# A tiny transfer out of the newest accumulated weight tile, put ahead of the transposing transfer of each feed-forward block

## The chip, the core and the metric

The program runs on one core of one Trainium2 chip. The metric is device time in microseconds (us): 1848.22 us, the median of three runs of the kernel before (1848.09, 1848.22 and 1849.85).

## What is computed

A two-layer encoder over 512 tokens of width 1024, in float32. Each layer adds half a gated feed-forward (width 2816) to x, then a mixer, then half a second feed-forward; a last norm closes it.

```python
def swiglu(x, w_in, w_out):
    gu = x @ w_in
    g, u = jnp.split(gu, 2, axis=-1)
    return (jax.nn.silu(g) * u) @ w_out

for l in range(DEPTH):
    x = x + 0.5 * swiglu(rms_norm(x, ffn1_norm[l]), ffn1_w_in[l], ffn1_w_out[l])
    x = x + mixer(rms_norm(x, mix_norm[l]), ...)
    x = x + 0.5 * swiglu(rms_norm(x, ffn2_norm[l]), ffn2_w_in[l], ffn2_w_out[l])
return rms_norm(x, final_norm)
```

The change lies in the four feed-forwards alone. The mixer (attention over a neighbourhood, a Fourier mix and their gates) has the same code before and after.

## The kernel before

**Products.** A product in float32 is made of three matmuls, on operands split into a high and a low part (`whi`, `wlo` for weights, `xh`, `xl` and the like for activations). ACT makes the high part (L191, L186), DVE the low part (L194, L187), TensorE multiplies (L514, L515, L517).

**Blocks.** The first half of a feed-forward works through the hidden width in five blocks (`NB`) of 512 columns (the first feed-forward has a plain part ahead of them; the other three begin with `first_block`, which carries 256 extra columns). A block is a two by two scheme of the Strassen and Winograd kind with seven products, in the order 1, 5, 6, 2, 7, 3, 4. Its four weight quarters are called a, b, c and d; a and b belong to the gate, c and d to the other factor. Products 5 and 7 want sums of quarters, d+c and c+a. The second half of the feed-forward (the output stage, tiles `o`) multiplies by the second weight matrix in the same scheme, in three chunks.

**Weights.** A quarter comes in two granules of 128 x 1024 (512 KB). `Raw.load` asks for a granule: SP issues the plain load into a `raw` tile (L148), and where a sum is wanted, GpSimd (POOL) issues an accumulating load of the second quarter into the same tile (L150), which has to wait until the plain load has landed. Below, "accumulating load" means the latter. The list of granules is fixed; `Stream` keeps eight of them (`FETCH`) asked for ahead of the last one that is split, and splits two (`AHEAD`) ahead of the product that is being issued. Nine `raw` buffers are in use.

**The hidden tile.** A block gives two half tiles of the hidden activation, `z2` (tokens 256 to 511) and `z1` (tokens 0 to 255), which are needed transposed. ACT pulls the two 16-bit words of each number apart into `zs` (`words_apart`, L350); SP issues a transposing transfer from `zs` to `zt` (`turned_words`, L356); one block later ACT joins the words into `at` (`joined_words`, L369), the one of `z2` after product 6, the one of `z1` after product 7. So SP's queue holds plain loads and transposing transfers, in an order that the scheduler made from the program, and each row of it waits on SP for its semaphores before it is issued; what stands behind it waits too.

**The function that the change replaces.** In `stage_ffn` the transposing transfer of `z2` stands under `with behind_sums(...)`. That function looks up the second granule of quarter c of the next block in the table `sums`; if that granule has been asked for, it issues a transfer of 16 numbers out of its tile to DRAM (tile `seen`), and `tc.issue_after` keeps what is issued under the `with` behind that transfer on the queue. Where the granule has not been asked for yet (`raw.t is None`), it does nothing. In the program as built, no row of SP's queue writes `seen`.

Of the kernel before, what the change touches and what calls it, by code (L numbers as in the profile page):

```python
# [9 lines left out]
F32 = mybir.dt.float32  # L10
# [81 lines left out]
def encoder_kernel(  # L92
    ctx: ExitStack, tc: tile.TileContext, xin, xtr, wst, gains, gfin, gbias, bias_in, dft, chan, ident_in, rot, out
):
    nc = tc.nc
# [8 lines left out]
    dp = ctx.enter_context(tc.tile_pool(name="dp", bufs=2, space=bass.MemoryType.DRAM))  # L104
# [3 lines left out]
    def nm(s):  # L108
        uid[0] += 1
        return f"{s}_{uid[0]}"  # L110

    def slot(dt=F32, s="k", shape=(4, 256)):
        return kp.tile([P, *shape], dt, tag="k", name=nm(s), bufs=23)
# [25 lines left out]
    class Raw:  # L139
# [3 lines left out]
        def load(self, parts=1):  # L143
            if self.t is None:
                self.t = raw_pool[0](self.n)
                for c in range(0, self.n, self.n // parts):
                    cs = slice(c, c + self.n // parts)
                    nc.sync.dma_start(out=self.t[:, cs], in_=wst[GRAN_AT[self.key]][:, cs])  # L148
                if self.plus:
                    G.dma_start(out=self.t, in_=wst[GRAN_AT[self.plus]][:, 0 : self.n], accum_op=ALU.add)  # L150

    class Item:
# [43 lines left out]
                G.dma_start(out=t, in_=wst[GRAN_AT[self.then]][:, 0:n], accum_op=ALU.add)  # L196
            self.out = (hi, lo)

    sums = {}

    def stage_items():
        items, st = [], 0

        def add(*a, **k):
            items.append(Item(*a, stage=st, **k))

        def strassen(s, name, idx, sizes, order, dma=False, behind=None):
            def key(q, g):
                return (s, name(q), idx, g) if g < 2 else (s, "h" + q, idx, 0)

            r = {}
            for q, q2 in (("a", None), ("b", None), ("c", "a"), ("d", "c")):
                r[q] = [Raw(key(q, g), n, q2 and key(q2, g)) for g, n in enumerate(sizes)]
                sums.update({z.key: z for z in r[q] if z.plus})
            d2 = [Raw(key("d", g), n) for g, n in enumerate(sizes)]
            at = [(m, g) for m in order for g in range(len(sizes))]
            if len(sizes) == 3:
                at.remove((2, 2))
                at.insert(at.index((7, 2)), (2, 2))
            for m, g in at:  # L220
                a, b, c, d = [r[q][g] for q in "abcd"]
                if m == 1:
                    add(a, neg=True)
                elif m == 2:
                    add(b)
                elif m == 3:
                    add(d, None if dma else b)
                elif m == 4:
                    add(d2[g])
                elif m == 5:  # L230
                    add(d)
                elif m == 6:
                    add(d, a, then=b.key if dma else None)
                else:
                    add(c)
                for key in (behind or {}).get(m, ()) if g == len(sizes) - 1 else ():
                    add(Raw(key))

        def out_sizes(c):
            return (1024, 512) if c == 0 else (1024, 1024)  # L240

        def ffn(s):
            first = not items
            if first:
                for g in range(4):
                    add(Raw((s, "cl", g)), parts=2 if g < 2 else 1, pieces=2 if g == 0 else 1)
            for j in range(NB):
                order = (1, 2, 5, 6, 7, 3, 4) if first and j == 0 else (1, 5, 6, 2, 7, 3, 4)
                strassen(s, lambda q: q, j, (1024,) * (2 if first or j else 3), order)
            for order in ((1,), (2,), (5, 6, 7, 3), (4,)):  # L250
                for c in range(3):
                    summed = s == (L - 1, 2) and c == 2
                    strassen(s, lambda q: "o" + q, c, out_sizes(c), order, summed)

        for l in range(L):
            ffn((l, 1))
            st += 1
            s = (l, 0)
            two = (1024, 1024)
            qk = [(s, "qk", g) for g in range(8)]  # L260
            strassen(s, lambda q: "u" + q, 0, two, (1, 5, 6, 2, 3, 7, 4), True, behind={5: qk[0:1], 6: qk[1:2], 2: qk[2:3], 3: qk[3:4], 7: qk[4:5]})
            for key in qk[5:] + [(s, "f", g) for g in range(4)]:
                add(Raw(key))
            st += 1
            for g in range(2):
                add(Raw((s, "n", 0, g)))
            st += 1
            for i in range(2):
                strassen(s, lambda q: "g" + q, i, two, ORDER, True)
            for g in range(2):  # L270
                add(Raw((s, "n", 1, g)))
            strassen(s, lambda q: "w" + q, 0, two, ORDER, True)
            ffn((l, 2))
        return items
# [78 lines left out]
    def turned_words(s):  # L353

        t = slot(U16, "zt", (2, 4, 256))
        nc.sync.dma_start_transpose(  # L356
            out=t.rearrange("p h q (b t) -> p (h q b) t", b=2), in_=s.rearrange("p h q b f -> p (h q b f)")
        )
        return t

    def apart(z):

        return turned_words(words_apart(z))
# [257 lines left out]
    def stage_ffn(norm, nxt, late):  # L621

        hx, lx = norm.h, norm.l
        stage = (norm.idx // 3, 1 + (norm.idx % 3) // 2)
        at = {}

        def at_tile(h, j, c):
# [20 lines left out]
        raw = norm.raw  # L648
# [51 lines left out]
        def halves(z, j, f0):  # L700

            turned.append((apart(z), j, f0))

        def behind_sums(jb):

            raw = sums.get((stage, "c", jb, 1))
            if raw is None or raw.t is None:
                return nullcontext()
            seen = dp.tile([16], F32, tag="seen", name=nm("seen"))
            to = bass.AP(tensor=seen.tensor, offset=seen.offset, ap=[[16, 1], [1, 16]])  # L710
            return tc.issue_after(nc.sync.dma_start(out=to, in_=raw.t[0:1, 0:16]))

        def joined():

# [107 lines left out]
        def first_block():  # L822
# [53 lines left out]
            half_times(h2, r2, hsb, hsb, 1)  # L876
            z2 = words_apart(z2)
            product(pa, acts[4], K4, False, again=True)
            with behind_sums(1):
                turned.append((turned_words(z2), 1, f0))  # L880
            times(z1, pa, 0)
            halves(z1, 0, f0)
# [3 lines left out]
        if not first:  # L886
            R = slot(F32, "R", (2, T))[:, 0, :]
            first_block()
        for jb in range(0 if first else 1, NB):
# [39 lines left out]
            if jb == NB - 1:  # L929
                make(2)  # L930
            product(pa, acts[4], K4, False, again=True)
            with behind_sums(jb + 1):
                turned.append((turned_words(z2), 1, f0))
            times(z1, pa, 0)
            halves(z1, 0, f0)
# [916 lines left out]
    norm = Norm(0)  # L1852
# [12 lines left out]
    for l in range(L):  # L1865
        nxt = Norm(3 * l + 1)
        stage_ffn(norm, nxt, False)
        norm, nxt = nxt, Norm(3 * l + 2)
        stage_mixer(l, norm, nxt)
        norm, nxt = nxt, Norm(3 * l + 3)  # L1870
        stage_ffn(norm, nxt, l == L - 1)
        norm = nxt
# [148 lines left out]
```

## Time and profile before

| what | value |
|---|---|
| runs | 1848.09, 1848.22, 1849.85 us; median 1848.22 |
| the profiled execution | 1848.85 us, span 1847.1 us, granted clock 0.999 |
| TensorE matmul (PE) busy | 1835.1 us, 99% of the span |
| DVE, ACT, POOL busy | 1602.5, 1312.4, 173.1 us |
| plain loads of 512 KB, issue to landing | 468, median 5.8 us |
| accumulating loads of 512 KB, issue to landing | 176, median 8.0 us |
| transposing transfers | 44 (40 of them in the feed-forwards), median 5.6 us |

The profile is one execution, so a sum made from it is held against its 1848.85 us, of which 1.75 us lie outside the span. A matmul of 512 columns starts every 0.227 us when nothing holds it, though its modelled length is 0.39 us, so the busy time of PE hides gaps of up to about 0.16 us. The weight loads (PEld) don't overlap one another and serve as a second witness. Landing times of single transfers are read by narrowing the view of a tile to a short window.

### The profile page before, as it was taken

What the parts mean: (1) busy time and instruction counts of PE and PEld (TensorE: products, weight loads), DVE (VectorE), ACT (ScalarE), POOL (GpSimd) and SP (SyncE); (2) the same over time, 40 slices, a digit from 0 to 9 for tenths busy, and PEclk for the clock granted to TensorE, in tenths of its full rate; (3) what the DMA queues carried; (4) which work ended last, traced back from release to release, by engine and by line L of the source; (5) the groups of instructions that cost most, each with busy time, mean ns of one, the idle gap of its engine ahead of it and who ended that gap; (6) DMA issues with size and microseconds to landing.
All of it is one profiled execution on the core that took longest, in us unless ns stands there. A gap on an engine that the chain in (4) does not pass through costs nothing.

```text
span 1847.1 us, 24562 instructions
## 1 busy us (share of the span) xinstructions
PE 1835.1 (99%) x8850; PEld 1528.9 (83%) x8850; DVE 1602.5 (87%) x1942; ACT 1312.4 (71%) x1777; POOL 173.1 (9%) x212
## 2 busy tenths in 40 slices
PE   9999999999999999999999999999999999999998
PEld 7888887888888888888888888888888888888886
DVE  7878899877989987889998888997869899888898
ACT  6777875668576767787667777766676776777865
POOL 0001011100111001001010100101001101010010
PEclk9999999999999999999999999999999999999999
DMA  9888798933896789979878887989258977999795
GB/s 300 226 231 222 192 270 270 218 131 113 231 233 180 171 218 236 220 198 278 250 193 218 224 218 199 277 285 217 69 179 208 232 180 178 226 217 218 203 278 162
DMA packets 198282, 395.72 MB, mean 214 GB/s; under 512 B 103760, under 2 KB 103888, under 8 KB 198160
## 3 DMA queue, kind: packets, MB, share of 16 engines
q1 hardware_dynamic: 168912, 294.23, 50.3%
q0 software_dynamic: 28816, 99.38, 30.3%
q8 instruction: 69, 1.13, 0.3%
q10 hardware_dynamic: 432, 0.55, 0.1%
q14 instruction: 53, 0.43, 0.1%
HBM read 367.88 MB, written 2.11 MB: 200 GB/s over the span
## 4 chain that ended last, share of the span: by engine, by line
PE 91%; DVE 4%; DMA 2%; issue 2%; ACT 1%; POOL 0%; SPq 0%; DVEq 0%; ACTq 0%; POOLq 0%
PE A L514 10%; PE A L517 10%; PE A L515 10%; PE o L517 5%; PE o L514 5%; PE o L515 5%; PE B L515 5%; PE B L514 5%; PE B L517 5%; PE ps L319 4%; PE ps L320 3%; PE ps L321 3%; PE C L515 3%; PE C L517 3%; PE C L514 3%
## 5 line engine op out<-in xcount | busy, mean ns | idle before, releaser
L194 DVE TENSOR_TENSOR wlo<-raw,whi 128x1024 fp32r<-128x1024 f32 (+1 forms) x532 | 628.2, 1190 | 174.0 <-ACT whi L191 171.5
L191 ACT ACTIVATE whi<-raw 128x1024 fp32r<-128x1024 f32 (+1 forms) x532 | 544.2, 1033 | 265.3 <-PE A L515 57.1
L150 POOL DMA_DIRECT2D raw<-in_wst_dram x166 | 144.3, 889 | 1343.0 <-DMA raw<-in_wst_dram 502.4
L164 DVE TENSOR_TENSOR raw<-raw,raw 128x1024 f32<-128x1024 f32 (+1 forms) x148 | 176.0, 1189 | 2.0
L515 PE MATMUL A<-whi,xl 128*128 128x512 f32 x400 | 155.7, 389 | 0.0
L514 PE MATMUL A<-whi,xh 128*128 128x512 f32 x400 | 155.7, 389 | 0.0
L369 ACT ACTIVATE at<-zt 128x1024 uint16<-128x1024 uint16 (+2 forms) x96 | 110.2, 1166 | 13.8 <-DMA zt<-zs 13.8
L186 ACT ACTIVATE whi<-raw 128x1024 fp32r<-128x1024 f32 (+1 forms) x83 | 85.3, 1035 | 46.1 <-issue 12.5
L517 PE MATMUL A<-wlo,xh 128*128 128x512 f32 x400 | 115.0, 389 | 0.0
L187 DVE SCALAR_TENSOR_TENSOR wlo<-raw,whi 128x1024 fp32r<-128x1024 f32 (+1 forms) x83 | 98.2, 1191 | 12.4 <-ACT whi L186 12.4
L517 PEld LDWEIGHTS A<-wlo,xh 128*128 128x128 f32 x400 | 75.1, 188 | 15.6
L515 PEld LDWEIGHTS A<-whi,xl 128*128 128x128 f32 x400 | 75.1, 188 | 15.5
L514 PEld LDWEIGHTS A<-whi,xh 128*128 128x128 f32 x400 | 75.1, 188 | 15.4
L515 PE MATMUL C<-whi,xl 128*128 128x512 f32 x208 | 81.0, 389 | 0.0
L515 PE MATMUL B<-whi,xl 128*128 128x512 f32 x208 | 81.0, 389 | 0.0
L514 PE MATMUL C<-whi,xh 128*128 128x512 f32 x208 | 80.9, 389 | 0.0
L514 PE MATMUL B<-whi,xh 128*128 128x512 f32 x208 | 80.9, 389 | 0.0
L350 ACT ACTIVATE zs<-th 128x1024 uint16<-128x1024 uint16 x80 | 79.5, 1042 | 0.4 <-DVE th L753 0.4
L746 ACT ACTIVATE th<-sn,rh 128x512 f32<-128x512 f32 x80 | 55.1, 716 | 34.0 <-DVE sn L589 33.2
L584 ACT ACTIVATE sn<-A 128x512 f32<-128x512 f32 x104 | 59.1, 584 | 24.2 <-PE A L517 24.2
L517 PE MATMUL C<-wlo,xh 128*128 128x512 f32 x208 | 59.8, 389 | 0.0
L517 PE MATMUL B<-wlo,xh 128*128 128x512 f32 x208 | 59.8, 389 | 0.0
(428 smaller groups left out, 4679.0 us busy)
## 6 DMA issues: line engine op xcount, KB each, us to landing
raw<-in_wst_dram SPq DMA_DIRECT2D x468, 512.0 KB, 5.8
raw<-in_wst_dram POOLq DMA_DIRECT2D x176, 512.0 KB, 8.0
bm<-in_bias_dram SPq DMA_DIRECT2D x16, 512.0 KB, 4.1
raw<-in_wst_dram SPq DMA_DIRECT2D x30, 256.0 KB, 4.5
x<-in_xin_dram SPq DMA_DIRECT2D x4, 512.0 KB, 10.2
raw<-in_wst_dram POOLq DMA_DIRECT2D x8, 256.0 KB, 9.3
dft<-in_dft_dram POOLq DMA_DIRECT2D x8, 256.0 KB, 10.9
gb<-in_gbias_dram SPq DMA_DIRECT2D x4, 512.0 KB, 9.4
```

Source lines behind the costliest of these rows:

```text
L150: G.dma_start(out=self.t, in_=wst[GRAN_AT[self.plus]][:, 0 : self.n], accum_op=ALU.add)
L164: V.tensor_tensor(self.raw.t, self.raw.t, self.add.t, ALU.add)
L186: S.activation(hi, t, AF.Copy, scale=-1.0)
L187: self.last = V.scalar_tensor_tensor(lo, t, -1.0, hi.bitcast(F32), ALU.mult, ALU.subtract)
L191: S.activation(hi[:, cs], t[:, cs], AF.Copy)
L194: self.last = V.tensor_tensor(lo[:, cs], t[:, cs], hi[:, cs].bitcast(F32), ALU.subtract)
L319: PE.matmul(ps, lh, rh, start=start, stop=False, skip_group_check=again)
L350: S.activation(s[:, h], words[:, h], AF.Copy)
L369: S.activation(to[:, w], t[:, w], AF.Copy)
L514: PE.matmul(ps, lh, rh, start=start, stop=False, skip_group_check=again)
L515: PE.matmul(ps, ll, rh, start=False, stop=False, skip_group_check=again)
L517: PE.matmul(ps, lh, rl, start=False, stop=stop, skip_group_check=again)
```

## The change

`behind_sums` and its table go. In their place `Raw.load` notes each granule for which it issues an accumulating load in `newest_sum[0]`, and `behind(newest_sum[0])`, at the same two places of `stage_ffn`, issues the transfer of 16 numbers out of the tile noted last. A granule that has been asked for always has a tile, so the transfer is now there in every block: twenty rows of SP's queue that were not there (five in each of four feed-forwards). Each waits on SP until the accumulating load into its tile has landed.

```diff
@@ class Raw, load
                 if self.plus:
+                    newest_sum[0] = self
                     G.dma_start(out=self.t, in_=wst[GRAN_AT[self.plus]][:, 0 : self.n], accum_op=ALU.add)
@@
-    sums = {}
+    newest_sum = [None]
@@ strassen
-                sums.update({z.key: z for z in r[q] if z.plus})
@@
+    def behind(raw):
+
+        if raw is None or raw.t is None:
+            return nullcontext()
+        seen = dp.tile([16], F32, tag="seen", name=nm("seen"))
+        to = bass.AP(tensor=seen.tensor, offset=seen.offset, ap=[[16, 1], [1, 16]])
+        return tc.issue_after(nc.sync.dma_start(out=to, in_=raw.t[0:1, 0:16]).ins)
@@ stage_ffn
-        def behind_sums(jb):
-
-            raw = sums.get((stage, "c", jb, 1))
...
-            return tc.issue_after(nc.sync.dma_start(out=to, in_=raw.t[0:1, 0:16]))
@@ first_block
-            with behind_sums(1):
+            with behind(newest_sum[0]):
                 turned.append((turned_words(z2), 1, f0))
@@ the loop over blocks
-            with behind_sums(jb + 1):
+            with behind(newest_sum[0]):
                 turned.append((turned_words(z2), 1, f0))
```

The instructions of PE, DVE, ACT and POOL stand in the same order before and after; only the numbers of the semaphores that they wait for differ. On SP's queue the twenty rows are added and the other rows keep their order. Three places show what they stand between (numbers behind names are buffer and serial numbers, and shift with each added tile).

SP's queue around the third block of the first feed-forward, before: the two transposing transfers are those of the third block's `zs`, `raw_231` and `raw_239` are the two granules of c+a of the block after it.

```order
L148 DMA raw_231_1276<-in_wst_dram 128x1024
L148 DMA raw_239_1306<-in_wst_dram 128x1024
L148 DMA raw_249_1364<-in_wst_dram 128x1024
L356 DMA_TRANSPOSE zt_234_1295<-zs_227_1255 128x16x128
L148 DMA raw_253_1385<-in_wst_dram 128x1024
L356 DMA_TRANSPOSE zt_236_1302<-zs_235_1299 128x16x128
```

The same place after the change: `raw_233` is the granule that was `raw_231`.

```order
L148 DMA raw_233_1280<-in_wst_dram 128x1024
L148 DMA raw_242_1312<-in_wst_dram 128x1024
L148 DMA raw_252_1370<-in_wst_dram 128x1024
L367 DMA seen_236_1299<-raw_233_1280 1x16
L356 DMA_TRANSPOSE zt_237_1301<-zs_229_1259 128x16x128
L148 DMA raw_256_1391<-in_wst_dram 128x1024
L356 DMA_TRANSPOSE zt_239_1308<-zs_238_1305 128x16x128
```

Here one row stands directly ahead of the transposing transfer, and waits for the first of the two accumulating loads.

SP's queue around the fourth block of the first feed-forward, after the change (before, the rows are the same without the two of `seen`): `raw_289` and `raw_298` are the two granules of c+a of the fifth block.

```order
L148 DMA raw_289_1587<-in_wst_dram 128x1024
L148 DMA raw_298_1619<-in_wst_dram 128x1024
L148 DMA raw_308_1677<-in_wst_dram 128x1024
L367 DMA seen_292_1606<-raw_289_1587 1x16
L367 DMA seen_356_1922<-raw_298_1619 1x16
L356 DMA_TRANSPOSE zt_293_1608<-zs_285_1566 128x16x128
```

The scheduler put the fifth block's row up here too, so that this transposing transfer stands behind both accumulating loads.

SP's queue at the end of `first_block` of the second feed-forward, after the change (before, the same without `seen`): `raw_1140` is the second granule of d+c of the next block, `raw_1161` and `raw_1167` are the two of its c+a, each with an accumulating load of its own.

```order
L148 DMA raw_1140_5929<-in_wst_dram 128x1024
L148 DMA raw_1151_6011<-in_wst_dram 128x1024
L148 DMA raw_1154_6029<-in_wst_dram 128x1024
L367 DMA seen_1157_6047<-raw_1140_5929 1x16
L148 DMA raw_1161_6058<-in_wst_dram 128x1024
L148 DMA raw_1167_6094<-in_wst_dram 128x1024
L148 DMA raw_1177_6152<-in_wst_dram 128x1024
L356 DMA_TRANSPOSE zt_1158_6049<-zs_1150_6008 128x16x128
```

Here three plain loads stand between the added row and the transposing transfer. The third and fourth feed-forward show the same.

More of the change, by code (lines that the diff above doesn't have):

```diff
@@ L623, in stage_ffn @@
         hx, lx = norm.h, norm.l
-        stage = (norm.idx // 3, 1 + (norm.idx % 3) // 2)
         at = {}
@@ L702, in halves @@
             turned.append((apart(z), j, f0))
-        def behind_sums(jb):
-            raw = sums.get((stage, "c", jb, 1))
[L707 to L710, printed above, removed]
-            return tc.issue_after(nc.sync.dma_start(out=to, in_=raw.t[0:1, 0:16]))
         def joined():
```

## The prediction

> **What bounds the kernel now.** I read the page first, then the busy time of the engines by stretches, then what SP's queue waits for, then the transposing transfers.
>
> ```profile
> PE 1835.1 (99%) x8850; PEld 1528.9 (83%) x8850; DVE 1602.5 (87%) x1942; ACT 1312.4 (71%) x1777; POOL 173.1 (9%) x212
> core 0: us, PE busy (x) PEld busy (x) DVE busy (x) ACT busy (x) POOL busy (x), PEclk, DMA share, GB/s
> 0.00:40.00 40.00, 37.52 (x156) 28.41 (x157) 30.22 (x46) 28.66 (x48) 3.79 (x8) 1.00 0.97 324
> 40.00:240.00 200.00, 200.00 (x887) 165.39 (x886) 168.21 (x190) 150.65 (x178) 15.48 (x18) 1.00 0.83 217
> 240.00:320.00 80.00, 79.28 (x358) 64.49 (x357) 77.75 (x81) 51.68 (x66) 10.85 (x13) 1.00 0.96 278
> 1160.00:1240.00 80.00, 80.00 (x366) 66.50 (x365) 78.88 (x82) 50.85 (x65) 10.81 (x13) 1.00 0.93 275
> 1520.00:1760.00 240.00, 240.00 (x1147) 202.14 (x1146) 206.18 (x224) 181.19 (x216) 20.93 (x25) 1.00 0.85 210
> 1800.00:1840.00 40.00, 38.64 (x170) 31.30 (x168) 37.93 (x53) 23.33 (x32) 3.44 (x4) 1.00 0.53 157
> 1840.00:1847.10 7.10, 0.00 (x0) 0.00 (x0) 2.93 (x11) 2.35 (x5) 0.00 (x0) 0.77 0.58 222
> ```
>
> TensorE is the bound. Its idle time is 1847.1 - 1835.1 = 12.0 us, and 2.5 (first row) + 1.4 + 7.1 (last two rows) = 11.0 of it lie ahead of the first block and behind the last. In the blocks of the first and the last feed-forward (40 to 240 and 1520 to 1760 us) it is busy throughout, as it is in those of the other two. The weight loads, which show short gaps too, agree: 165.39 / 200 = 0.827 in the first feed-forward's blocks, 66.50 in 80 us of the third one's output stage, but 64.49 in the first one's: 2.0 / 0.83 = 2.4 us are lost there. So TensorE has next to nothing to win from better transfers. What the change can do is starve it.
>
> ```profile
> SPq L148 <- DVE wlo L194: 725.2, 295, 18.1
> SPq L356 <- ACT zs L350: 114.2, 11, 13.5
> L356 SPq DMA_TRANSPOSE zt<-zs x44: 1356/3568/7882, 72.6 to 1740.0; - x44
>   DMA zt<-zs: 13.8, 8
> DMA to landing us min/median/max: 4.3/5.6/10.4
> ```
>
> SP waits for buffers most of the time, and its transposing transfers wait for ACT (up to 13.5 us at once): a wait for a transfer that has landed by then costs nothing. Who waits for a transposed tile is ACT, 8 times, 13.8 us in all; no PE row names it.
>
> **The change part by part.** Nothing is removed that took time (no row of `seen` before). *Twenty issues on SP*: a row of L148 takes 0.33 us, 20 x 0.33 = 6.6 us of a queue that waits over 700 us for buffers: 0 on the path, except directly ahead of a transposing transfer. There I count 0.6 us, the distance of the two SP rows below at 150.72 and 151.34.
>
> *Third block, four times.* Here ACT waits for the transposed tiles, so here a delay is passed on.
>
> ```profile
> 139.34 0.86 POOL L150 DMA_DIRECT2D raw<-in_wst_dram  x1 [4.64 <-DMA raw<-in_wst_dram]
> DMA to landing us min/median/max: 7.8/7.8/7.8
> 146.95 3.67 SPq L356 DMA_TRANSPOSE zt<-zs  x1
> 150.72 0.53 SPq L148 DMA_DIRECT2D raw<-in_wst_dram  x1
> 151.34 3.82 SPq L356 DMA_TRANSPOSE zt<-zs  x1
> 157.20 0.49 ACT L369 ACTIVATE at<-zt 128x256 uint16<-128x256 uint16 x1 [2.69 <-DMA zt<-zs]
> 158.37 1.04 ACT L191 ACTIVATE whi<-raw 128x1024 fp32r<-128x1024 f32 x1
> 160.49 0.39 PE L514 MATMUL C<-whi,xh 128*128 128x512 f32 x1
> 163.21 0.39 PE L514 MATMUL C<-whi,xh 128*128 128x512 f32 x1
> ```
>
> The accumulating load issued at 139.34 lands at 139.3 + 7.8 = 147.1; the transposing transfer went out at 146.95. It now goes out at about 147.1 + 0.6 = 147.7, 0.8 us late, and the second one behind it too. ACT's wait of 2.69 us becomes up to 3.5. What hides it: the high part that ACT makes next ends at 158.37 + 1.04 = 159.41, and PE takes it at 160.49, so 1.08 us are to spare. The last of the four:
>
> ```profile
> L150 POOL DMA_DIRECT2D raw<-in_wst_dram x1: 860/860/860, 1651.4 to 1651.4; - x1
> DMA to landing us min/median/max: 8.9/8.9/8.9
> 1660.01 3.75 SPq L356 DMA_TRANSPOSE zt<-zs  x1
> ```
>
> Its load lands at 1651.4 + 8.9 = 1660.3, and the transposing transfer, issued at 1660.01, goes out at 1660.9 instead. The two between, read alike, come out 0.2 and 0.8 us late. Delays 0.8, 0.2, 0.8 and 0.9 us. For the cover of the other three I take that of the first, 1.08, as their place in the program is the same. Sum: 0. Bounds: at best 0 (ACT's wait already costs PE nothing); with the cover gone, all of it, 0.8 + 0.2 + 0.8 + 0.9 = 2.7 us.
>
> *Fourth block, four times*: behind both accumulating loads, the later wait decides.
>
> ```profile
> 1694.67 0.86 POOL L150 DMA_DIRECT2D raw<-in_wst_dram  x1 [0.45 <-DVE wlo L187]
> DMA to landing us min/median/max: 8.6/8.6/8.6
> 1698.09 4.46 SPq L356 DMA_TRANSPOSE zt<-zs  x1
> 1710.96 1.36 ACT L369 ACTIVATE at<-zt 128x1024 uint16<-128x1024 uint16 x1
> ```
>
> This is the worst of the four: 1694.7 + 8.6 = 1703.3, + 0.6 = 1703.9, 5.8 us late. With the median landing of 5.6 us the tile is there at 1709.5, and ACT asks for it at 1710.96: 1.5 us of cover. Plain loads behind it on SP slip by as much. A granule lasts PE 163.21 - 160.49 = 2.72 us, and eight are asked for ahead: 21.8 us, against a landing of 5.8 plus the slip of 5.8. Sum: 0.
>
> *First block of the last three feed-forwards*: three plain loads are held, two of which get accumulating loads.
>
> ```profile
> 650.97 0.85 POOL L150 DMA_DIRECT2D raw<-in_wst_dram  x1 [0.39 <-issue]
> DMA to landing us min/median/max: 10.7/10.7/10.7
> 653.67 0.33 SPq L148 DMA_DIRECT2D raw<-in_wst_dram  x1
> 664.82 0.85 POOL L150 DMA_DIRECT2D raw<-in_wst_dram  x1 [0.29 <-issue]
> DMA to landing us min/median/max: 5.6/7.3/9.1
> 684.48 1.99 ACT L191 ACTIVATE whi<-raw 128x1024 fp32r<-128x1024 f32 x2
> raw<-in_wst_dram SPq DMA_DIRECT2D x468, 512.0 KB, 5.8
> ```
>
> The load at 653.67 now waits until 651.0 + 10.7 = 661.7, + 0.6: 8.6 us late. It lands 5.8 us later (the median of such loads, in the last row) at 668.1, and the accumulating load, which went out at 663.7, follows at 668.1 or a little later: 4.4 us late. The second of the pair landed at 664.8 + 9.1 = 673.9 and now lands near 678.3; ACT takes the pair from 684.48, its second at 685.5: 7 us to spare. Sum: 0, and even a slip of the full 8.6 would end at 682.5.
>
> *Less overlap of the two kinds of transfers.* At the end of this first block a transposing transfer ran beside two accumulating loads:
>
> ```profile
> L356 SPq DMA_TRANSPOSE zt<-zs x2: 2105/4994/7882, 665.8 to 673.8; - x2
> DMA to landing us min/median/max: 4.4/7.1/9.9
> ```
>
> Beside them it took 9.9 us, without them 4.4. The Trainium skill, page "DMA: Bandwidth & Descriptors", section "Queues, rings and completion order", says that each transfer engine takes turns between the queues that have work, a packet at a time: by it a transposing transfer beside an accumulating load is slowed, not stopped, and waiting for the load's landing instead can only be later. The two landings agree that it is slowed; by that rule the sum keeps its sign or gets worse. The gain that the separation can give is bounded by the idle time above: 2.4 us in the first output stage.
>
> Sum: 0 of 1848.85 us. Against the runs shown, whose median is 0.6 us lower, and with a little for the two third blocks that have 0.2 us left, I say **1848.4 us**. A measurement of this kernel tells a difference of about 0.2%, 3.7 us, from none.
>
> **The rivals.**
>
> *The tiny transfer's own landing counts too.* If the transposing transfer starts only when the tiny one ahead of it has landed, it is later by one small transfer; the nearest row is
>
> ```profile
> vs<-v SPq DMA_DIRECT2D x8, 128.0 KB, 2.3
> ```
>
> 2.3 us. The third blocks are then 3.1, 2.5, 3.1 and 3.2 us late and pass on what is over 1.08: 2.0 + 1.4 + 2.0 + 2.1 = 7.5 us, and the time is 1848.4 + 7.5 = 1855.9. It decides from a delay of about 1.1 us in the third block; anything that costs as much there (a longer issue, a later accumulating load) counts the same. Against it: the transposing row carries no wait for that transfer. For it: no row shows a tiny transfer in this queue, and the cover is thin at a place that comes four times. Slower, chance 0.21. The same page, section "Anatomy of one DMA", says that transfer engines don't wait on semaphores, the issuing sequencer does; by it this rival falls away, and no run shows it yet.
>
> *Held loads reach PE in the first block.* If the slip of 8.6 us comes through in full and the pair of accumulating loads, now beside the transposing transfers, takes 10.7 us instead of 9.1, the second lands at 682.5 + 1.6 = 684.1; ACT asks at 685.5. One more microsecond and a half, and three feed-forwards each lose what is over, some 1 to 2 us: 1851.4 to 1854.4. Chance 0.07; it counts as slower for the most part.
>
> *The output stage of the first feed-forward gains.* Freed transfers end its stall: 1848.4 - 2.4 = 1846.0. Against it: the last row added ahead of it stands some 50 us before (the fourth block), and loads there wait for buffers. Chance 0.06, within 0.2%.
>
> *The change does next to nothing*, since in many blocks the accumulating load has landed before ACT hands over `zs`. The time is the forecast's, and it is counted there.
>
> **How the numbers follow.** Forecast 0.62, the slower rivals 0.21 and 0.07, the gain 0.06, unexplained 0.04, all of it faster by over 0.2%, which the idle time all but excludes. Same: 0.62 + 0.06 = 0.68. Slower: 0.21 + 0.07 = 0.28. Faster: 0.04. The range goes from the gain's 1846.0 to the first rival's 1855.9; the forecast's own is 1846.0 to 1851.1 (its bound of 2.7 us above).
>
> **What would show it.** Right: twenty tiny transfers; PE without idle in the stretches of the blocks, with weight loads near 0.83 to 0.84 of the time; ACT's waits for transposed tiles up from 13.8 us by 2 to 4; SP waiting for accumulating loads. Wrong: rows in which PE or a weight load waits for `whi` or `wlo` near 160, 758, 1077 and 1673 us (the first rival), or near 685 (the second), or weight loads over 66 us in 240 to 320 (the gain).

## The result and the profile after

The changed kernel takes 1859.28 us (median of 12 runs, 1850.42 to 1874.61), the kernel before beside it 1848.39 us (1846.24 to 1854.80): a ratio of 1.0056, 95% interval 1.0031 to 1.0081. A second measurement gave 1859.25 us and 1.0059 (1.0039 to 1.0080). It is slower, by nearly three times what a measurement can tell, and its runs spread over 24 us, where those of before spread over 9. The ratios here and below come from the single runs, not from the medians, and leave out the one run of all these kernels that is in the slow state (1883.15 us, of the kernel called "the same again" below). The forecast (1848.4 us, range to 1855.9) was wrong.

The profiled run of the changed kernel is one of its quicker ones: 1855.0 us, span 1853.2. (The lines of the changed code have moved: L148 and L356 are the same, L150 is now L151, L191 L192, L369 L377, L514 L522; L367 is the tiny transfer.) First the page's engines, then the same stretches as before, with three short ones added:

```profile
PE 1838.2 (99%) x8850; PEld 1529.5 (83%) x8850; DVE 1601.9 (86%) x1942; ACT 1312.1 (71%) x1777; POOL 173.1 (9%) x212
core 0: us, PE busy (x) PEld busy (x) DVE busy (x) ACT busy (x) POOL busy (x), PEclk, DMA share, GB/s
40.00:240.00 200.00, 200.00 (x887) 165.44 (x886) 168.19 (x191) 150.45 (x178) 15.51 (x18) 1.00 0.85 218
240.00:320.00 80.00, 80.00 (x366) 66.50 (x366) 79.78 (x82) 52.87 (x67) 10.85 (x13) 1.00 0.97 279
680.00:700.00 20.00, 19.40 (x86) 15.74 (x85) 11.72 (x13) 13.87 (x16) 1.70 (x2) 1.00 1.03 269
1000.00:1020.00 20.00, 19.73 (x88) 16.01 (x86) 11.72 (x13) 14.20 (x17) 1.71 (x2) 1.00 1.08 270
1160.00:1240.00 80.00, 79.57 (x361) 65.07 (x360) 78.52 (x82) 49.76 (x63) 10.82 (x13) 1.00 0.95 272
1600.00:1610.00 10.00, 8.31 (x37) 6.58 (x36) 3.91 (x5) 6.74 (x8) 0.18 (x1) 1.00 1.05 313
1800.00:1840.00 40.00, 37.93 (x164) 30.04 (x163) 35.46 (x44) 21.37 (x28) 3.47 (x4) 1.00 0.56 153
```

TensorE still has no gap in the blocks of the first feed-forward. The new gaps lie near 687, 1006 and 1604 us: the second block of the second, third and fourth feed-forward, the one behind `first_block`. The stall of before in 240 to 320 us is gone (66.50 us of weight loads against 64.49). What they wait for, from the waits of the whole run (in all, times, longest):

```profile
PE A L522 <- ACT whi L192: 2.5, 3, 1.7
...
ACT at L377 <- DMA zt<-zs: 22.5, 10, 3.9
```

ACT and TensorE at the last of the three, from the timeline:

```profile
1602.13 1.37 ACT L377 ACTIVATE at<-zt 128x1024 uint16<-128x1024 uint16 x1 [3.87 <-DMA zt<-zs]
1605.03 2.93 ACT L192 ACTIVATE whi<-raw 128x1024 fp32r<-128x1024 f32 x3
...
1606.11 0.50 PE L522 MATMUL A<-whi,t7h 128*128 128x512 f32 x1 [1.69 <-ACT whi L192]
```

ACT, which works in order, waits 3.87 us for the transposed tile, so it makes the next high part late, and TensorE waits for that. Why the tile is late stands in the timeline of SP and POOL, here at the first of the three places:

```profile
659.13 0.26 SPq L367 DMA_DIRECT2D seen<-raw  x1
659.48 1.31 SPq L148 DMA_DIRECT2D raw<-in_wst_dram  x3
664.24 18.26 SPq L356 DMA_TRANSPOSE zt<-zs  x2
...
663.91 0.86 POOL L151 DMA_DIRECT2D raw<-in_wst_dram  x1 [12.51 <-DVE th L751]
665.10 0.85 POOL L151 DMA_DIRECT2D raw<-in_wst_dram  x1 [0.33 <-issue]
```

How long these took, from the view of the accumulating loads' line and that of the tile `zt`, both narrowed to this stretch:

```profile
DMA to landing us min/median/max: 6.1/11.8/17.5
...
DMA to landing us min/median/max: 18.6/18.6/18.6
```

The three held plain loads go out together, behind the tiny transfer. The transposing transfer (664.24) now goes out between the two accumulating loads of c+a (663.91 and 665.10; "the pair" below), and it takes 18.6 us, the second load 17.5 us; before, it went out 1.0 us behind both loads (665.81 against 664.82), and they took 9.9 and 9.1. The same landing rows read 18.3 and 15.7 in the third feed-forward, 19.7 and 19.3 in the fourth. While they stand in each other's way, little is moved (the last two columns are the transfer engines' busy share and GB/s):

```profile
670.00:682.00 12.00, 12.00 (x54) 9.94 (x53) 8.27 (x7) 6.02 (x8) 0.00 (x0) 1.00 1.29 80
```

The share says that the transfer engines are busy throughout, at 80 GB/s, where a stretch of 5 us just before and one just behind have 161 and 268. It counts the time that packets take, not what they bring: SP's queue has 1637 packets of 256 bytes here, 102 ns each in the mean, where the profile before has 1881 of them in the 2 us from 674, with only transposing transfers under way, 20 ns each. I call this the jam.

Pairing the 8850 matmuls of the two profiles one to one, the three gaps are worth 0.9, 0.6 and 2.0 us, 3.5 of the 6.1 us between the spans. Of the rest, 2.0 us are won near 300 us and 4.2 lost in the output stages of the third and fourth feed-forward. Neither is charged to the change: 1.6 and 2.0 us are also won in the two profiles of the kernel below that leaves the first feed-forward as it was, and the kernel with the loop's rows alone lost 3.1 us in those two output stages of its profile and is not slower.

### The profile page after: what moved, and what is told of

It is laid out like the page before. It is cut to its first block, busy times and chain, and to the rows that moved or that the text cites. A ratio compares the mean times of both kernels' runs of the same rounds, so it can differ in the third digit from the quotient of the medians.

```text
span 1853.2 us, 24603 instructions
## 1 busy us (share of the span) xinstructions
PE 1838.2 (99%) x8850; PEld 1529.5 (83%) x8850; DVE 1601.9 (86%) x1942; ACT 1312.1 (71%) x1777; POOL 173.1 (9%) x212
## 4 chain that ended last, share of the span: by engine, by line
PE 94%; DMA 3%; DVE 1%; ACT 1%; issue 0%; SPq 0%; ACTq 0%; DVEq 0%
PE A L522 10%; PE A L525 10%; PE A L523 10%; PE o L525 7%; PE o L522 7%; PE o L523 7%; PE B L522 5%; PE B L523 5%; PE B L525 5%; PE ps L319 4%; PE ps L320 3%; PE ps L321 3%; DMA zt<-zs 3%; PE C L523 2%; PE C L522 2%; PE C L525 2%
## 5 line engine op out<-in xcount | busy, mean ns | idle before, releaser
L192 ACT ACTIVATE whi<-raw 128x1024 fp32r<-128x1024 f32 (+1 forms) x532 | 543.4, 1033 | 258.0 <-PE A L523 51.6
L151 POOL DMA_DIRECT2D raw<-in_wst_dram x166 | 144.3, 892 | 1348.1 <-DMA raw<-in_wst_dram 773.1
L522 PE MATMUL A<-whi,xh 128*128 128x512 f32 x400 | 155.7, 389 | 0.0
L377 ACT ACTIVATE at<-zt 128x1024 uint16<-128x1024 uint16 (+2 forms) x96 | 110.3, 1166 | 22.6 <-DMA zt<-zs 22.5
L522 PEld LDWEIGHTS A<-whi,xh 128*128 128x128 f32 x400 | 75.1, 188 | 15.4
L522 PE MATMUL C<-whi,xh 128*128 128x512 f32 x208 | 80.9, 389 | 0.0
L522 PE MATMUL B<-whi,xh 128*128 128x512 f32 x208 | 80.9, 389 | 0.0
## 6 DMA issues: line engine op xcount, KB each, us to landing
x<-in_xin_dram SPq DMA_DIRECT2D x4, 512.0 KB, 10.2
dft<-in_dft_dram POOLq DMA_DIRECT2D x8, 256.0 KB, 10.6
gb<-in_gbias_dram SPq DMA_DIRECT2D x4, 512.0 KB, 10.2
```

The lines of the kernel that those rows point to most:

```text
L192: S.activation(hi[:, cs], t[:, cs], AF.Copy)
L377: S.activation(to[:, w], t[:, w], AF.Copy)
L522: PE.matmul(ps, lh, rh, start=start, stop=False, skip_group_check=again)
```

## The experiments

Theory: the loss is made by the three tiny transfers in `first_block`, through the jam. Rivals: the seventeen in the loop cost; waiting for an accumulating load costs; holding the plain loads costs.

**Which rows cost.** The loop's alone, then those of `first_block` alone; the second twice, the second time beside the changed kernel.

```diff
 # first_block (loop alone) / the loop over blocks (first_block alone)
-            with behind(newest_sum[0]):
-                turned.append((turned_words(z2), 1, f0))
+            turned.append((turned_words(z2), 1, f0))
```

> The tiny transfers stay in the loop over blocks (17 of them) and go from first_block (3). Theory: the loss is made in first_block, where the transposing transfer now goes out between the two accumulating loads of the next block's c+a, and it and the second load then take 16 to 20 us instead of 9 to 11. So here the first transposing transfer of these blocks takes 9 to 11 us again, TensorE shows no gap near 687, 1006 and 1603 us, and the time is that of before, 1847 to 1850 us. Rival: the rows in the loop cost in the output stages (1.4 us near 1190 to 1226 and 2.9 us near 1820 to 1835 in the profile after, less 2.0 won near 300); then 1850 to 1853 us.

> Only the three tiny transfers in first_block stay; the loop over blocks is as before. Theory: the transposing transfers of the three first blocks take 18 to 20 us, ACT waits for them 2 to 4 us each, TensorE loses 0.6 to 2.1 us behind each: 3.6 us in all and what it draws after it, 1852 to 1859 us. Rival (the rows in the loop cost it): 1847 to 1850 us.

> The kernel with the three tiny transfers in first_block alone, again, beside the changed one. 1851 to 1860 us as the changed one if the rows in first_block are the whole cause, some 1853 against 1859 if not.

> The changed kernel once more, for a second profile and to have it on one chip with the kernel that has only the rows in first_block (1853.0 us, ratio 1.0024). If the rows in first_block are the whole cause, the two agree within their intervals here, 1851 to 1860 us both; if the rows in the loop add to it, this one is slower by 3 us or more. In its profile at least one of the three first blocks shows a transposing transfer of 16 to 20 us with both accumulating loads issued within 1 us of it, and TensorE a gap of 0.5 to 2 us behind each of those.

Loop alone: 1849.24 us, ratio 1.0002 (0.9994 to 1.0011). `first_block` alone: 1853.01 us, 1.0024 (1.0010 to 1.0037), then 1860.21 us, 1.0052 (1.0032 to 1.0072); the changed kernel beside that one 1859.25, 1.0059. Side by side on one chip the two agree within their intervals, and the loop's rows alone cost nothing, so the three rows in `first_block` are the cause, as far as these intervals tell. The two measurements of `first_block` alone differ (runs at 1847.63 to 1862.55, and at 1847.82 to 1883.15); that its runs jam more or less often would explain it, but is not shown, as only one run of each was profiled, the first time one of the quicker ones (1849.46 us). In the second profile of the changed kernel, with a span of 1867.6 us, the jam in the second feed-forward is at its worst. First the landings of `zt` and of the pair, then the stretch, then ACT and TensorE in the timeline:

```profile
DMA to landing us min/median/max: 30.3/30.3/30.3
...
DMA to landing us min/median/max: 27.5/28.2/29.0
```

```profile
670.00:693.00 23.00, 15.86 (x70) 12.79 (x69) 7.85 (x7) 5.59 (x8) 0.00 (x0) 0.94 1.26 59
```

```profile
694.11 1.34 ACT L377 ACTIVATE at<-zt 128x1024 uint16<-128x1024 uint16 x1 [14.41 <-DMA zt<-zs]
...
698.07 0.80 PE L522 MATMUL A<-whi,t7h 128*128 128x512 f32 x1 [12.21 <-ACT whi L192]
```

One transposing transfer takes 30.3 us, the two loads beside it 27.5 and 29.0, at 59 GB/s; TensorE stands still for 12.21 us. Paired with the profile before, this gap is worth 15.1 us and one of the same kind in the third feed-forward 5.4: together the 20.5 us by which the spans differ (what is won and lost elsewhere cancels). In this profile the jam is the whole loss.

**Waiting or holding.** In the next two, both transposing transfers of `first_block` go out one product later, behind a tiny transfer out of the second granule of c+a, so behind the whole pair. The second of the two kernels also keeps the tiny transfer that holds the three plain loads.

```diff
 # first_block
-            with behind(newest_sum[0]):
-                turned.append((turned_words(z2), 1, f0))
             times(z1, pa, 0)
-            halves(z1, 0, f0)
+            apart_only.extend([(z2, 1, f0), (words_apart(z1), 0, f0)])
 # two(), between products 1 and 5 of the next block
+            if apart_only:
+                with behind(newest_sum[0]):
+                    for s, j, f0 in apart_only:
+                        turned.append((turned_words(s), j, f0))
+                apart_only.clear()
 # the second kernel only, in first_block
+            behind(newest_sum[0])
```

> In first_block the two transposing transfers are issued later in the program, in the next block between its products 1 and 5, behind a tiny transfer out of the second granule of c+a: behind both accumulating loads. Theory (it is the order of transposing transfer and second accumulating load that costs): the loads land about 10 us after issue or sooner, the transposing transfers then take 4.3 to 5 us each, the first landing near 677 of the 681.6 us at which ACT asks; no gap in TensorE near 687, 1006, 1603: 1846 to 1850 us. Rival (waiting for an accumulating load is itself what costs, as the transfers go out some 8 us later): ACT waits for the first transposed tile 1 to 4 us, and the time is 1851 to 1858 us.

> The three plain loads in first_block are held behind the tiny transfer as in the changed kernel, but the two transposing transfers go out behind the pair of accumulating loads (a second tiny transfer, out of the second granule of c+a). Theory (the coincidence costs, the hold itself nothing): transposing transfers of 4.3 to 5 us, no gap in TensorE near 687, 1006, 1603, 1846 to 1850 us. Rival (the hold costs): the loss stays, 1852 to 1860 us.

Without the hold 1848.07 us, ratio 1.0000 (0.9991 to 1.0009); with it 1848.37 us, 1.0001 (0.9992 to 1.0009). In the second feed-forward of the first kernel, the transposing transfer issued at 671.5 lands in 4.5 us and the loads in 7.2 and 7.4; in the second kernel SP's rows in the timeline are

```profile
659.27 0.25 SPq L367 DMA_DIRECT2D seen<-raw  x1
659.61 1.30 SPq L148 DMA_DIRECT2D raw<-in_wst_dram  x3
673.42 0.24 SPq L367 DMA_DIRECT2D seen<-raw  x1
673.76 4.54 SPq L356 DMA_TRANSPOSE zt<-zs  x2
```

The plain loads are held as in the changed kernel, the transposing transfer goes out 9.5 us later than there (673.76 against 664.24), and nothing is lost. So neither the hold nor the wait costs by itself.

**One load of the pair left out.** The changed kernel without the second accumulating load, in the last three feed-forwards (that quarter then lacks its addend).

```diff
+                second = self.key[1:] == ("c", 1, 1) and self.key[0] != (0, 1)
-                if self.plus:
+                if self.plus and not second:
```

> The changed kernel without the second of the two accumulating loads of c+a of the block behind first_block, in the last three feed-forwards (three loads of 180; that quarter then lacks its addend). The plain loads are held and the tiny transfers stand as in the changed kernel. Theory (it takes the pair): with one load issued within 1 us of the transposing transfer, that takes 6 to 11 us, no gap in TensorE near 687, 1006, 1603: 1846 to 1850 us. Rival (one load beside it is enough, or the hold costs): transposing transfers of 15 us and more, 1851 to 1860 us.

1848.81 us, ratio 1.0005 (0.9992 to 1.0019); the transposing transfers, still issued within 1 us of the first load, take 9.6, 8.4 and 9.3 us. In the profiled run, one of the quick ones, there is no jam, and the loss is no longer clear of noise. Two of the 11 runs, 1856.57 and 1858.73 us, are still long and were not profiled, so it is open whether one load can jam too, seldom.

**The pair moved, without any hold.** Seven kernels have the loop's rows alone and move the pair against the transposing transfer by small operations on GpSimd: a copy of 8 columns out of the plain load's tile and fills of a scratch tile, ahead of the first load or of the second, in different numbers. These lines are from the one called "second later" in the table.

```diff
+                    if self.key[1:3] == ("c", 1) and self.key[0] != (0, 1):
+                        with tc.issue_after(newest_sum[0].ins):
+                            if self.key[3] == 0:
+                                G.tensor_copy(scratch, self.t[:, 0:8])
+                            for _ in range(3):
+                                idle = G.memset(scratch, 0.0)
+                        hold = tc.issue_after(idle.ins)
...
+                    with hold:
+                        self.ins = G.dma_start(
...
```

The expectations stand in the order of the table's rows, from "fills ahead of the second load" to "second later".

> As the kernel with the tiny transfers in the loop alone, but GpSimd fills a small scratch tile 32 times (some 3 us) ahead of the second accumulating load of c+a of the block behind first_block, so that this load goes out after the transposing transfer; no plain load is held. Theory (the order costs): the transposing transfer and the second load take 15 to 20 us, TensorE has gaps near 687, 1006 and 1603 us, 1851 to 1859 us. Rival (what costs in the changed kernel are the three plain loads held behind the tiny transfer): the transposing transfer takes 9 to 11 us, 1847 to 1850 us.

> As the kernel with the tiny transfers in the loop alone (1849.2 us), but GpSimd does 17 small operations (some 2.8 us) ahead of the first accumulating load of c+a of the block behind first_block, once its plain load has landed, so that the pair goes out at the time of the transposing transfer: the first within 1 us before it, the second within 1 us behind it. No plain load is held and no tiny transfer stands in first_block. Theory now (what costs is that all three start within about a microsecond; a second load 2 us behind the transposing transfer did not cost): in at least one of the three blocks the transposing transfer takes 15 to 20 us, TensorE gaps of 0.5 to 2 us behind it, 1850.5 to 1859 us. Rival (the three held plain loads cost): 1847 to 1850 us, transposing transfers of 7 to 11 us.

> As the kernel with the tiny transfers in the loop alone, but GpSimd does 4 small operations (some 2.5 us) ahead of the first accumulating load of c+a of the block behind first_block. With 17 operations the pair went out 1.7 to 3.6 us behind the transposing transfer, too late for the test; 13 fills of 0.16 us fewer bring it 2.1 us forward, so that in the third and fourth feed-forward the second load goes out 0 to 1.5 us behind the transposing transfer. No plain load is held and no tiny transfer stands in first_block. Theory (a second accumulating load issued 0 to 1.6 us behind the transposing transfer jams both): in at least one block whose second load falls into that stretch it takes 15 to 22 us, and TensorE has a gap behind it; the time is 1850 to 1858 us if two or three fall in, 1848 to 1850 if one or none. Rival (the held loads are needed too): loads of 7 to 11 us even where it falls into the stretch.

> As the kernel in which the pair went out at the time of the transposing transfer without any held load (first load 0.2 to 0.5 us ahead of it, second 0.1 to 0.4 us behind: loads of 11 to 17 us, no time lost), but with 5 fills of 0.16 us between the two loads, so that the second goes out 0.6 to 1.3 us behind the transposing transfer, as in the changed kernel (0.5 to 0.9). Theory (it is this order and distance alone, not the hold): jams of 16 to 20 us and more in at least two of the three blocks, gaps in TensorE behind them, 1850.5 to 1860 us. Rival (the held plain loads are needed for the long jam): loads of up to 17 us again and 1847 to 1850.5 us.

> The same with 4 more fills ahead of the first load, so that the pair goes out 0 to 0.5 us and 1 to 2 us behind the transposing transfer, as in the second profile of the changed kernel, whose jams were the longest (21 and 30 us). Theory: jams of 18 to 30 us, gaps in TensorE, 1852 to 1865 us. Rival (the held plain loads are needed): 1847 to 1850.5 us.

> No held load, no tiny transfer in first_block; GpSimd's operations set the pair so that the first load goes out some 0.4 us ahead of the transposing transfer and the second 0.6 to 1.3 us behind it (one fill between them). Theory (the distance alone decides): second loads of 15 us and more in at least two blocks and 1850 to 1858 us. Rival (the held plain loads add to it): second loads of at most 17 us, no gap in TensorE, 1847 to 1850 us.

> No held load and no tiny transfer in first_block; the first load of the pair 0.4 us ahead of the transposing transfer, the second 1 to 1.4 us behind it (3 fills between them). If the distance alone made the long jams of the changed kernel, the second loads take 15 us and more and the time is 1850 us and up; if the held loads are needed, 10 to 14 us and 1847 to 1850 us.

Several of them missed the distance that they were built for (17 operations took 4.3 us in the second feed-forward, not 2.8, as the copy took 1.74 to 3.12). Together they cover 0.1 to 3.6 us, with nothing between 0.4 and 1.3 us, where the first profile of the changed kernel lies (0.5 to 0.9). For each kernel, from its one profile: how far behind the first transposing transfer the second load went out in the three places (minus: ahead), and how long the second load took.

| kernel | second load, us behind | it took, us | ratio (95%) |
|---|---|---|---|
| before | -1.0, -2.4, -2.3 | 9.1, 9.9, 11.0 | 1 |
| loop alone | -2.5, -1.9, -2.3 | 8.2, 8.9, 10.1 | 1.0002 (0.9994 to 1.0011) |
| fills ahead of the second load | 2.2, 1.9, 2.6 | 6.9, 7.7, 6.0 | 1.0000 (0.9991 to 1.0009) |
| both late | 3.6, 2.2, 2.2 | 17.7, 9.1, 8.7 | 0.9998 (0.9989 to 1.0007) |
| pair at the transfer | 0.1, 0.1, 0.4 | 16.6, 14.1, 10.9 | 1.0004 (0.9995 to 1.0013) |
| pair spread | 3.0, 1.6, 1.6 | 9.8, 11.5, 10.2 | 0.9991 (0.9981 to 1.0001) |
| pair behind | 2.2, 2.3, 2.2 | 9.6, 9.2, 9.6 | 0.9997 (0.9986 to 1.0008) |
| middle | 0.1, 0.2, 0.1 | 15.9, 13.9, 13.2 | 1.0002 (0.9993 to 1.0010) |
| second later | 1.3, 1.3, 1.3 | 12.3, 12.7, 11.7 | 0.9999 (0.9991 to 1.0008) |
| changed, first profile | 0.9, 0.8, 0.5 | 17.5, 15.7, 19.3 | 1.0056 (1.0031 to 1.0081) |
| changed, second profile | 1.3, 1.6, 0.6 | 29.0, 19.9, 14.7 | 1.0059 (1.0039 to 1.0080) |
| first_block alone | -0.9, 0.3, 2.7 | 8.3, 18.4, 9.8 | 1.0024 (1.0010 to 1.0037) |
| the same again | 1.5, 0.0, 1.4 | 10.6, 22.3, 19.7 | 1.0052 (1.0032 to 1.0072) |

(17.7 in "both late" was beside the second transposing transfer, 0.3 us ahead of the load; that tile is asked for later.) The coincidence alone slows the second load to 11 to 17 us, where the second is issued within half a microsecond behind the transposing transfer, and costs no time: the theory that it is enough fell here. The slack can account for that: in these seven profiles ACT waits 0.9 us at most for this tile, and TensorE has no gap behind it. ACT asks for the tile 15.8 us after the transposing transfer goes out when nothing holds it up; in the timeline of the kernel with the loop's rows alone:

```profile
663.65 9.51 SPq L356 DMA_TRANSPOSE zt<-zs  x2
...
679.42 1.36 ACT L377 ACTIVATE at<-zt 128x1024 uint16<-128x1024 uint16 x1
```

At like distances the held loads mostly make the difference: at 1.3 us the second load took 12.3, 12.7 and 11.7 us without them and 29.0 with them, at 1.6 us 11.5 and 10.2 against 19.9. But at 1.5 us with them ("the same again") it took 10.6: not every block with held loads jams. The experiments ran on five chips, each beside the kernel before. On two of these chips both kinds were measured: one without held loads that lost nothing ("middle", "second later") and one with them that lost time (the two variants of the next part).

**The hold kept, the jam disturbed.** Two variants of the changed kernel: 10 fills ahead of the second load; and the third of the held plain loads put behind the transposing transfer.

```diff
 # first variant, ahead of the second accumulating load
+                            for _ in range(10):
+                                idle = G.memset(scratch, 0.0)
 # second variant: turns holds the transposing transfers issued so far
+                late = self.key[1:] == ("d", 1, 0) and not self.plus and self.key[0] != (0, 1)
+                with tc.issue_after(turns[-2]) if late else nullcontext():
```

> The changed kernel with all its tiny transfers and held loads, but 10 fills on GpSimd ahead of the second accumulating load of c+a of the block behind first_block, so that it goes out 1.8 to 3 us behind the transposing transfer and no longer 0.5 to 1.6. Theory (the distance decides): second loads of 7 to 12 us, transposing transfers of at most 12, no gap in TensorE near 687, 1006, 1603, 1847 to 1850 us. Rival (the held loads decide): loads of 15 us and more, 1852 to 1862 us.

> The changed kernel with all its tiny transfers, but the third of the three held plain loads (not wanted for 20 us) put behind the transposing transfer of z2 instead of ahead of it, so that it is not under way beside the pair of accumulating loads. Theory now (the held loads start together and are still under way when the pair and the transposing transfer start): with a third of them gone the transposing transfers take at most 16 us and the time is 1847 to 1851 us. Rival (the distance of the pair alone): no change against the changed kernel, 1853 to 1861 us.

First variant: second loads 3.6, 1.2 and 2.2 us behind, taking 12.9, 15.8 and 11.7 us; 1848.92 us, ratio 1.0033 (1.0009 to 1.0057), seven runs at 1846 to 1849 and five at 1858 to 1865. Second variant: 0.3 and 0.9 us behind and 0.6 ahead, taking 17.3, 9.8 and 7.1 us; 1849.35 us, 1.0013 (1.0001 to 1.0025). The second variant takes away most of the loss, but not clearly all of it. The interval of the first overlaps that of the changed kernel, so it is open whether it takes any away.

What is shown: the loss needs the transposing transfer beside the pair (pair ahead: no loss; one load less: none clear of noise) and the held plain loads, issued together a few microseconds ahead (no hold: no loss at any distance tried; two held loads in place of three: about a quarter of it). How the held loads lengthen the jam stays open; the landings of two of the three are not in the trace. Their packets are (4096 bytes each, those of a transposing transfer 256): in the six blocks of the changed kernel's two profiles the last plain one ends 0.9 to 2.4 us behind the issue of the transposing transfer, in "pair at the transfer", "middle" and "second later" between 0.8 us ahead of it and 0.2 behind. So the held loads are still moving when the pair and the transposing transfer start, and are done long before the jam ends. That is not enough for a jam: in the block at 1.5 us named above they move for 2.0 us behind the issue too.

No version beats the kernel before: the lowest ratio, 0.9991 (0.9981 to 1.0001), reaches 1.

## Why the prediction was wrong

- *What bounds the kernel*: right. TensorE had nothing to win, and the change could only starve it.
- *Twenty issues on SP*: right, and smaller than counted. The tiny transfer and the transposing one are 0.35 us apart (the rows below), not 0.6.
- *Third block*: right, sum 0. In the first feed-forward SP's rows in the timeline are

```profile
147.40 0.26 SPq L367 DMA_DIRECT2D seen<-raw  x1
147.75 2.98 SPq L356 DMA_TRANSPOSE zt<-zs  x1
```

  and the page's row of all transposing transfers is

```profile
zt<-zs SPq DMA_TRANSPOSE x44, 4.4
```

  The transfer goes out at 147.75 (foretold: 147.7), 0.8 us late, but it takes 4.3 us in place of 5.8, so the tile is there no later. The second accumulating load is under way beside it both times. The row above has a landing for 28 of the 44 only, so its 4.4 can't be held against the 5.6 of before. The twelve transposing transfers of `z2` in the second, third and fourth blocks have one in both profiles: their median falls from 5.5 to 4.3 us. So the loop's rows do shorten these transfers, where TensorE does not wait for them.
- *Fourth block*: right. In the last feed-forward the transfer goes out at 1706.1, 8.0 us later, of which TensorE itself is 3.4 us late by then, and ACT does not wait.
- *First block of the last three feed-forwards*: this step failed. It followed the slip only to the held loads' own tiles: the pair 4.4 us late, "7 us to spare", sum 0. What happened there is that the transposing transfer came late, and TensorE lost 0.9, 0.6 and 2.0 us in the first profile, 15.1 and 5.4 in the second. The slip was sized too large against the profile it was read from: the first held load goes out 5.8 us late (659.48 for 653.67), not 8.6, as the load waited for landed in 8.6 us and not 10.7, and the pair 0.2 us late. That pair had come late by itself before, at 663.7; against the loop's rows alone (660.0) it is 3.9 us late. What the step left out is the transposing transfer beside the pair, whose tile ACT asks for first, with 5.9 us of slack (675.73 to 681.59). The rows of the profile before:

```profile
665.81 10.09 SPq L356 DMA_TRANSPOSE zt<-zs  x2
681.59 1.36 ACT L369 ACTIVATE at<-zt 128x1024 uint16<-128x1024 uint16 x1
```

  It also took landing times as fixed: 9.1 us for the second load, at worst 10.7, where 14.7 to 29.0 were seen, and the transposing transfer got no price at all.
- *Less overlap*: in `first_block` the tiny transfer brought more overlap, not less. There 9.9 against 4.4 us was on the page as the price beside two accumulating loads, and was used for a gain only. The rule of the Trainium skill that was set beside it (page "DMA: Bandwidth & Descriptors", section "Queues, rings and completion order": transfer engines take turns between queues, a packet at a time) led the prediction to "slowed, not stopped". The two landings of before agreed; the jam does not look like taking turns at full rate, with 59 and 80 GB/s at a share of 1.26 and 1.29, and the measurement decides.
- *First rival* (the tiny transfer's own landing counts): did not happen. The transposing transfer goes out 0.35 us behind the tiny one and lands 4.3 us later, where the median of all is 4.4.
- *Second rival* (held loads reach PE in the first block): right in place, "near 685", and in the last link, `whi` late on ACT; chance 0.07. It even has the pair "now beside the transposing transfers", but prices the loads alone (10.7 us). Its path was another (the accumulated tile, not the transposed one), so the place was right in part by luck, and its price too small: 1851.4 to 1854.4 us against 1859.3.
- *Third rival* (the first output stage gains): 2.0 us came, but came also where its feed-forward was unchanged, so this is not credited to the change.
- *ACT's waits* up by 2 to 4 us: they rose from 13.8 to 22.5 us in one profile and to 32.3 in the other. Of the 22.5, 9.1 are the three places of the jam. In the third blocks, where the rise was foretold, the longest wait rose from 2.7 to 3.3 us as said, but the sum was 13.4 in place of 13.8.

## What to carry to other kernels

When a row is put into an in-order queue, list not only what waits behind it but what the held work will meet when it is let go: here loads that had been spread over 8 us went out within 1, and the accumulating pair that follows them met a transposing transfer. Check the slack of every consumer at that place, the one with the least first, and against landing times under the new neighbours, not those of the profile before. An ordering edge that is good in one loop can be bad in the one block whose neighbours differ: look at which tile "the newest" is there.

## What the runs showed of the hardware

Transposing transfers and accumulating loads can slow one another far more than the bytes tell. A transposing transfer took 4.4 us alone, 9.9 beside a pair and 15.5 to 30.3 in the changed kernel's two profiles, at 59 and 80 GB/s in the jam, where the 5 us just behind it had 285 and 268.

A stall of TensorE costs more than its length once it is long enough. Second profile of the changed kernel, behind its 12.21 us of idle time, and the second profile of `first_block` alone, behind 4.29 us, and the first profile of the changed kernel, behind 1.69 us (the last columns are PEclk, DMA share, GB/s):

```profile
698.00:704.00 6.00, 5.93 (x15) 4.67 (x16) 5.83 (x6) 4.87 (x7) 1.62 (x2) 0.53 1.02 341
704.00:710.00 6.00, 6.00 (x28) 4.95 (x27) 4.35 (x5) 3.92 (x4) 0.09 (x1) 1.00 1.02 243
```

```profile
1009.00:1014.00 5.00, 4.98 (x13) 3.93 (x14) 5.00 (x6) 3.87 (x5) 0.82 (x1) 0.54 0.99 388
```

```profile
1606.00:1610.00 4.00, 3.89 (x17) 3.24 (x18) 3.91 (x5) 2.87 (x5) 0.18 (x1) 1.00 0.95 351
```

TensorE starts again at half its clock (0.53 and 0.54 in the mean of these stretches) and does 15 matmuls in 6 us in place of 28; the 1.69 us of the first profile (last row) cost no clock. Paired with the profile before, the two stalls are worth 15.1 and 6.7 us, 2.9 and 2.4 more than the idle time. Two shorter ones in the same two profiles, 3.67 and 3.84 us of idle time, cost the clock too and are worth 5.4 and 5.6 us. The Trainium skill says so (page "TensorE: Matmul & The Clock Gate", section "Part 1: The HAM clock gate (the "warmup" mystery)"): half rate after an idle window of some 3.4 us, full rate again after as long a busy one. The trace agrees: the window lies between 1.69 us, which cost no clock, and 3.67, which did; TensorE then ran 3.1 to 5.6 us at half rate.
